# In-projection and state space part woven with attention in steps of at most six products

## The chip, the cores and the metric

The kernel runs on one core of one Trainium2 chip. The core has five engines, each with its own queue of instructions that it works off in order: TensorE (PE, matrix products and transposes; its weight loads are shown apart as PEld), VectorE (DVE), ScalarE (ACT), GpSimd (POOL) and SyncE (SP), which here issues nearly all DMA transfers. Engines wait for each other by semaphores. The metric is the device time of one execution in microseconds (us); the time of a kernel is the median of its runs.

## The reference

Two layers of a transformer with 1024 tokens of width 1024, in float32. A layer modulates and normalises its input, multiplies it by w_in (2472 columns) and feeds three heads in parallel: differential attention (4 heads, q and k of width 32, v of width 64), latent attention (MLA, 4 heads, from a normalised c_q and c_kv) and a state space part (8 heads, state 64, a causal convolution of width 4 ahead of it, a gate z behind it). The three outputs are joined, multiplied by w_out and added to the input; then comes an MLP of 4096 with the square of relu.

```python
def _diff_attention(q, k, v, lam, subln_g, lambda_init):
    ...
        p = _masked_softmax(s1, mask) - lam * _masked_softmax(s2, mask)
        return jnp.einsum('bhqk,bkhe->bqhe', p.astype(v.dtype), v)
    ...
def _ssd_scan(xs, dt, a, bm, cm):
    ...
    scores = jnp.einsum('bclhn,bcshn->bhcls', cc, bc) * decay_in
    y_diag = jnp.einsum('bhcls,bcshp->bclhp', scores, xd)
    ...
    def step(state, inp):
        st, dec = inp
        return state * dec[..., None, None] + st, state
    ...
    y_off = jnp.einsum('bclhn,bchpn,bhcl->bclhp', cc, prev, jnp.exp(a_cs))
    return (y_diag + y_off).reshape(b, l, h, p)
```

## The kernel before

**Products.** A float32 product is made of three products of split operands (a high part and a remainder): `mm3` (L190 to L193) issues high by high, high by low and low by high into one PSUM bank. A bank of the in-projection holds 512 columns for 128 rows and sums over 8 tiles of 128, so it takes 24 products, and then ACT or DVE empties it.

**The part that is woven.** `mixer` runs the in-projection together with both attentions. Each of these is a Python generator that writes down instructions and, between them, yields a cost:

- `in_proj` writes q, k, v, then the columns for MLA (they go to HBM as the tensor d_c), then those of the state space part (xbc) with their convolution, up to the mark "pairs". Behind that comes the z loop over 8 tiles of 128 tokens: a bank of z columns, then `scores`, `first` and `second` of the state space part for that tile (L1255 are the Y products of `second`, L1263 those with the state, L1273 the new state). It reaches "hidden" ahead of the last `second`.
- `attention` goes through four heads of differential attention. Scores are L962 and L964, the softmax L896 and L897, the transposes of the probabilities L922, their products with v L909, the turned results L938. When a head is done, it is normalised (L987 to L991) and written to HBM (d_cc, L992).
- `mla` goes through the tiles t of 128 tokens: `first` loads the d_c rows of a tile (L1041), scales them on DVE (L1042, L1043) and transposes them on PE (L1046); `second` multiplies them by the up-projections (L1056, L1058); `third` transposes q and k (L1085). It also reads back the heads' and the state space part's outputs from d_cc (L1146, L1147). `load_wout` loads w_out in eight parts (L1288).

`weave` adds cost / rate to a stream's clock at each yield and lets the stream with the smallest clock go next. There are three weaves in a layer: up to "pairs" with the first two heads; the z loop with the other two heads and the head of MLA; and what is left of the z loop with the first scores of MLA and the load of w_out.

**What sets the order.** The generators set the order in which the program is written. The scheduler of the language then orders each engine's instructions again by its own estimate of when each can start, and that order is what the engines follow. All working tiles come from one arena in on-chip memory, given out in the order of writing: a place that was given back earliest is taken first. So when the order of writing changes, tiles get other places, and a load waits for whoever had its place last, all over the kernel.

**Behind the weave.** The output projection (L1324 to L1330: loads and stores of the residual) runs with MLA and is followed by the MLP. `renorm` normalises a tile and, for the tiles 4 to 7, makes transposes and several sums of them (`transp_late`, L212 on PE, L217 and L231 on DVE) for a Strassen-like product in the MLP. `mlp_up` first does six plain blocks (L315, L317: 24 products each, weights by six narrow loads of 128 columns, 0.5 MB, L270), beside which the last tiles are transposed, and then for each of 16 blocks the products of sums (`sums`), whose weights come by 1-MB loads of 256 columns (L270 again) and are added on POOL (L284 to L290). L230 and L231 split operands on ACT and DVE; L248 stores results to HBM.

The functions that the diff touches, and what calls them:

## Time and profile before

| | before |
|---|---|
| median of 3 runs | 2828.76 us (2823.73 to 2833.22) |
| the profiled execution | 2827.39 us |
| its span, from the first to the last instruction | 2825.7 us |
| PE busy | 2642.5 us, 94% |
| DVE, ACT, POOL busy | 1755.9, 1111.0, 587.5 us |
| mean granted clock of PE, as a share of full speed | 0.952 |

An engine is busy while it executes; register, branch and semaphore instructions and the issuing of DMAs do not count. The granted clock is what a throttle leaves PE of its full clock: a stretch is either at the full 2.4 GHz or at half of it, and a figure between is a mean over stretches. A row of the timeline names the line, the tile written and the tile read; a bracket behind it gives the time for which the engine stood idle just before and who released it.

### The profile page before, as it was taken

The page shows a single profiled execution, that of the slowest core. Times are in us where ns is not written, and L with a number is a line of the kernel's source. Part 1 is how long each engine was busy: PE and PEld are TensorE (multiplying, and loading weights), DVE is VectorE, ACT ScalarE, POOL GpSimd, SP SyncE. Part 2 cuts the span into 40 slices and gives each one's busy share as a digit, 9 for nine tenths or more (in the row PEclk, how much of TensorE's full clock was granted, in tenths as well). Part 3 has the DMA queues.
Part 4 walks back from the last instruction along what each step waited for, and adds up shares of the span by engine and source line. Part 5 has one row for each costly group of instructions (what it writes and reads, how often), then busy time and mean ns, then how long its engine had stood idle before and what let it go on. Part 6 is the DMA issues. An engine that isn't in the chain of part 4 may idle for free.

```text
span 2825.7 us, 34756 instructions
## 1 busy us (share of the span) xinstructions
PE 2642.5 (94%) x12530; PEld 2066.1 (73%) x12530; DVE 1755.9 (62%) x3223; ACT 1111.0 (39%) x2145; POOL 587.5 (21%) x517
## 2 busy tenths in 40 slices
PE   5799999899879999999999999988997999999998
PEld 4677776676757777777778777765766888888886
DVE  7767666544867777756585576664459654643435
ACT  5243443544534446121143433354445455621212
POOL 1441233310333220000021113342003522000002
PEclk9899988899989999999999998888998999999999
DMA  6441212322345546534331121132133432541313
GB/s 225 116 137 51 94 50 61 110 73 84 101 150 165 158 148 216 179 122 151 107 119 48 56 91 63 54 101 86 52 105 104 153 116 101 177 149 65 120 47 102
DMA packets 268527, 311.54 MB, mean 110 GB/s; under 512 B 28674, under 2 KB 212164, under 8 KB 268356
## 3 DMA queue, kind: packets, MB, share of 16 engines
q1 hardware_dynamic: 268356, 309.32, 34.0%
q8 instruction: 99, 1.62, 0.2%
q14 instruction: 72, 0.59, 0.1%
HBM read 242.85 MB, written 66.43 MB: 109 GB/s over the span
## 4 chain that ended last, share of the span: by engine, by line
PE 65%; DVE 11%; DMA 7%; issue 2%; ACT 2%; POOL 1%; SPq 0%; DVEq 0%; ACTq 0%; POOLq 0%
PE bank_b L191 9%; PE bank_b L193 9%; PE bank_b L192 9%; PE bank_s L191 8%; PE bank_s L192 8%; PE bank_s L193 8%; PE bank_s L962 3%; DVE split L231 2%; PE bank_a L909 2%; PE bank_t L922 2%; DVE arena_f L570 2%; DMA arena_f<-in_w_ada 1%; DMA d_r<-arena_f 1%; PE bank_s L656 1%; PE bank_a L938 1%
## 5 line engine op out<-in xcount | busy, mean ns | idle before, releaser
L191 PE MATMUL bank_b<-split 128*128 128x512 f32 (+2 forms) x1824 | 728.5, 400 | 51.0 <-ACT split L230 33.1
L192 PE MATMUL bank_b<-split 128*128 128x512 f32 (+2 forms) x1824 | 709.6, 389 | 3.5 <-DVE split L231 3.1
L193 PE MATMUL bank_b<-split 128*128 128x512 f32 (+2 forms) x1824 | 706.5, 389 | 2.9 <-DVE split L231 2.9
L230 ACT CAST split<-arena_f 128x512 fp32r<-128x512 f32 (+1 forms) x424 | 305.8, 747 | 678.3 <-PE bank_s L192 425.8
L191 PE MATMUL bank_s<-split 128*128 128x512 f32 (+2 forms) x1152 | 456.1, 398 | 18.3 <-DVE arena_f L390 6.7
L192 PE MATMUL bank_s<-split 128*128 128x512 f32 (+2 forms) x1152 | 451.2, 392 | 4.4 <-DVE split L231 1.8
L191 PEld LDWEIGHTS bank_b<-split 128*128 128x128 f32 x1824 | 354.1, 194 | 129.5 <-ACT split L230 34.8
L193 PE MATMUL bank_s<-split 128*128 128x512 f32 (+2 forms) x1152 | 448.2, 389 | 0.0
L231 DVE TENSOR_TENSOR split<-arena_f,split 128x512 fp32r<-128x512 f32 (+1 forms) x424 | 381.7, 919 | 92.8 <-ACT split L230 92.0
L193 PEld LDWEIGHTS bank_b<-split 128*128 128x128 f32 x1824 | 352.7, 193 | 71.6 <-DVE split L231 5.0
L192 PEld LDWEIGHTS bank_b<-split 128*128 128x128 f32 x1824 | 354.7, 194 | 68.5 <-issue 4.9
L408 DVE TENSOR_TENSOR arena_f<-arena_f,bank_s 128x1024 f32<-128x1024 f32 x126 | 153.5, 1218 | 230.9 <-PE bank_s L193 230.9
L191 PEld LDWEIGHTS bank_s<-split 128*128 128x128 f32 (+1 forms) x1152 | 218.4, 190 | 73.8 <-DVE arena_f L390 7.4
L192 PEld LDWEIGHTS bank_s<-split 128*128 128x128 f32 (+1 forms) x1152 | 219.5, 191 | 50.4 <-DVE split L231 3.5
L193 PEld LDWEIGHTS bank_s<-split 128*128 128x128 f32 (+1 forms) x1152 | 219.1, 190 | 43.4 <-issue 0.2
L897 ACT ACTIVATE arena_f<-bank_s,nm 128x128 f32<-128x128 f32 (+3 forms) x192 | 141.8, 740 | 191.8 <-DVE nm L896 160.8
L896 DVE TENSOR_REDUCE nm<-bank_s 128x1 f32<-128x128 f32 (+3 forms) x192 | 142.2, 752 | 118.8 <-PE bank_s L1111 64.5
L570 DVE SCALAR_TENSOR_TENSOR arena_f<-arena_f,cond 128x128 f32<-128x128 f32 x448 | 161.7, 387 | 71.4 <-DMA arena_f<-in_b_ada 32.9
L246 ACT ACTIVATE arena_f<-arena_f 128x512 f32<-128x512 f32 x128 | 80.8, 632 | 141.6 <-DVE arena_f L331 69.6
L962 PE MATMUL bank_s<-split 32*128 32x512 f32 (+3 forms) x576 | 124.0, 390 | 12.3 <-ACT arena_f L897 9.1
L925 ACT COPY arena_f<-bank_t 128x512 f32<-128x512 f32 (+1 forms) x160 | 86.8, 542 | 114.1 <-PE bank_t L922 100.9
L696 POOL TENSOR_TENSOR arena_f<-arena_f 128x1024 f32<-128x1024 f32 x14 | 33.6, 2399 | 454.0 <-ACT rstd_y L182 340.0
(281 smaller groups left out, 3207.0 us busy)
## 6 DMA issues: line engine op xcount, KB each, us to landing
arena_f<-in_w_ada SPq DMA_DIRECT2D x80, 512.0 KB
d_r<-arena_f SPq DMA_DIRECT2D x128, 256.0 KB
arena_f<-in_w_up SPq DMA_DIRECT2D x32, 1024.0 KB
arena_f<-in_w_down SPq DMA_DIRECT2D x64, 512.0 KB
arena_f<-d_r SPq DMA_DIRECT2D x64, 512.0 KB
arena_f<-d_x SPq DMA_DIRECT2D x36, 512.0 KB
d_x<-arena_f SPq DMA_DIRECT2D x23, 512.0 KB
arena_f<-in_w_in SPq DMA_DIRECT2D x20, 512.0 KB
```

Of the source, the lines that this page charges most:

```text
L191: mm(out, wh, xh, start=start, stop=False)
L192: mm(out, wh, xl, start=False, stop=False)
L193: mm(out, wl, xh, start=False, stop=stop)
L230: self.nc.scalar.copy(hi, src)
L231: (eng or self.nc.vector).tensor_sub(lo, src, f32(hi))
L246: nc.scalar.activation(t, t, AF.Relu)
L408: nc.vector.tensor_add(y[t], y[t], ps)
L570: nc.vector.scalar_tensor_tensor(acc, in0=w[:, k], scalar=self.cond[:, k:k + 1], in1=acc, op0=ALU.mult, op1=ALU.add)
L896: nc.vector.tensor_reduce(nm, S[:, 0:n], axis=AX.X, op=ALU.max, negate=True)
L897: nc.scalar.activation(p[:, 0:n], S[:, 0:n], AF.Exp, bias=nm, accum_out=ls)
L925: nc.scalar.copy(held, ps[:, 0:w])
L962: nc.tensor.matmul(S[mp][:, c0:c1], Q[rw, a, tok], K[rw, b, c0:c1], start=a == b, stop=a == 1 and c1 < n)
```

## The change

The products of an in-projection bank are no longer written in one piece. `feat_major` and `tok_major` become generators that yield 1.3 after every two of the eight tiles summed, that is after six products (`values` after twelve, at a quarter of the width). The yield after the bank falls from 5.1 to 1.2, so a bank costs 3 x 1.3 + 1.2 = 5.1 as before; the two yields of 4.6 of a d_c tile become 2.6. `second` yields 1.0 five times, of which four lie inside it, in place of 5.0 behind it. The part ahead of "attend" is not woven, and its background work is called at the same places as before. Two rates change: attention 80 to 76 in the second weave, the rest of the z loop 1 to 1000 in the third.

```diff
@@ feat_major, tok_major
     def feat_major(self, wt, m, hT, hf):
         ps = self.bank()
...
         for k in range(KD):
             self.mm3(ps, wt[:, 0, k, mm], wt[:, 1, k, mm], hT[0][:, k, sl], hT[1][:, k, sl], k == 0, k == KD - 1)
+            if k % 2 and k < KD - 1:
+                yield 1.3
         return ps

-    def tok_major(self, wt, hT, t, n):
-        ps = self.bank()[:, 0:n]
+    def tok_major(self, wt, hT, t, ps, step=2):
         sl = slice(t * P, t * P + P)
         for k in range(KD):
             self.mm3(ps, hT[0][:, k, sl], hT[1][:, k, sl], wt[:, 0, k], wt[:, 1, k], k == 0, k == KD - 1)
-        return ps
+            if (k + 1) % step == 0 and k < KD - 1:
+                yield 1.3
@@ qk, values
-                yield 5.1
+                yield 1.2
...
-                ps = self.tok_major(wt, hT, t, 256)
+                ps = self.bank()[:, 0:256]
+                yield from self.tok_major(wt, hT, t, ps, 4)
...
                 if t % 2:
                     next(bg, None)
-                    yield 5.1
+                yield 1.3
@@ in_proj: C_CQ tiles (twice), xbc, z loop
-            yield 4.6
+            yield 2.6
...
-                ps = self.feat_major(wt, m - m0, hT, hf)
+                ps = yield from self.feat_major(wt, m - m0, hT, hf)
...
-                yield 5.1
+                yield 1.2
...
-            for k in range(KD):
-                self.mm3(ps, hT[0][:, k, tok], hT[1][:, k, tok], wz[:, 0, k], wz[:, 1, k], k == 0, k == KD - 1)
+            yield from self.tok_major(wz, hT, t, ps)
             z = F.get(512)
...
-            yield 5.1
+            yield 1.2
             held = scores(t, held)
...
-            second(t, z, held)
-            yield 5.0
+            yield from second(t, z, held)
+            yield 1.0
@@ second
             for h in range(8):
                 nc.tensor.matmul(yd[:, h * 64:h * 64 + 64], L[:, h], xd[:, h], start=True, stop=True)
+                if h == 3:
+                    yield 1.0
             nc.vector.tensor_add(y, y, yd.rearrange("p (h e) -> p h e", e=64))
+            yield 1.0
...
                 F.put(xs)
+            yield 1.0
...
                 nc.vector.tensor_add(state, state, sp.rearrange("p (h e) -> p h e", e=64))
+            yield 1.0
@@ mixer
-        self.weave((80, da), (80, self.until(ip, "hidden")), (20, self.until(m, "hidden"), PRE))
-        self.weave((1, ip), (30, self.until(m, 0)), (WOW, self.load_wout(l, st)))
+        self.weave((76, da), (80, self.until(ip, "hidden")), (20, self.until(m, "hidden"), PRE))
+        self.weave((1000, ip), (30, self.until(m, 0)), (WOW, self.load_wout(l, st)))
```

In the changed kernel the lines from L900 on are about 5 higher, from L1279 on 10 higher: the load of d_c L1041 is L1046 there, the write of a head L992 is L997, the reads of d_cc L1146 and L1147 are L1151 and L1152, the write of the state space part L1279 is L1289, the load of w_out L1288 is L1298, the residual's stores and loads L1330 and L1346 are L1340 and L1356.

SP's queue in layer 1, where the weave ends and MLA begins, before (d_cc_116<-arena_f 128x8x64 is the write of head 3, the first 128x384 load of d_c behind it is that of tile 3):

```order
L1279 DMA d_cc_116<-arena_f 128x512
L1288 DMA arena_f<-in_w_out 128x1024 x3
L992 DMA d_cc_116<-arena_f 128x8x64
L1146 DMA arena_f<-d_cc_116 128x2x256
L1041 DMA arena_f<-d_c_114 128x384
L1146 DMA arena_f<-d_cc_116 128x2x256
L1147 DMA arena_f<-d_cc_116 128x2x512
L1041 DMA arena_f<-d_c_114 128x384
```

And after (the first two 128x384 loads belong to tiles 2 and 3, the pair to tiles 5 and 4):

```order
L1289 DMA d_cc_116<-arena_f 128x512
L1046 DMA arena_f<-d_c_114 128x384
L1298 DMA arena_f<-in_w_out 128x1024 x5
L1046 DMA arena_f<-d_c_114 128x384
L1289 DMA d_cc_116<-arena_f 128x512
L1298 DMA arena_f<-in_w_out 128x1024
L1152 DMA arena_f<-d_cc_116 128x2x512
L1046 DMA arena_f<-d_c_114 128x384 x2
L997 DMA d_cc_116<-arena_f 128x8x64
L1151 DMA arena_f<-d_cc_116 128x2x256
```

The loads of tiles 3, 4 and 5 have moved ahead of the write of the head. In layer 0 it is the other way round. SP's queue there before (the second 128x384 load is that of tile 3, the third that of tile 4):

```order
L1041 DMA arena_f<-d_c_113 128x384
L1288 DMA arena_f<-in_w_out 128x1024
L1041 DMA arena_f<-d_c_113 128x384
L1288 DMA arena_f<-in_w_out 128x1024 x3
L627 DMA arena_f<-d_mod 128x8x1
L1288 DMA arena_f<-in_w_out 128x1024
L992 DMA d_cc_115<-arena_f 128x8x64
L1041 DMA arena_f<-d_c_113 128x384
```

And after (the single 128x384 load is that of tile 5, the pair is tiles 3 and 4):

```order
L1289 DMA d_cc_115<-arena_f 128x512
L1046 DMA arena_f<-d_c_113 128x384
L561 DMA arena_f<-in_b_ada 1x128
L997 DMA d_cc_115<-arena_f 128x8x64
L1151 DMA arena_f<-d_cc_115 128x2x256
L1046 DMA arena_f<-d_c_113 128x384 x2
L1152 DMA arena_f<-d_cc_115 128x2x512
```

The load of tile 3 has moved behind the write of the head and its reading back.

SP's queue in layer 0 where the MLP begins, before (128x8x128 are the narrow loads, of which the first and the second row here are the fifth and the sixth; of the 128x8x256 loads the single one is block 1, the four are blocks 2, 0, 3 and 4):

```order
L270 DMA arena_f<-in_w_up 128x8x128
L248 DMA d_r_109<-arena_f 128x512 x3
L270 DMA arena_f<-in_w_up 128x8x128
L1330 DMA d_x_104<-arena_f 128x1024
L248 DMA d_r_109<-arena_f 128x512 x2
L270 DMA arena_f<-in_w_up 128x8x256
L248 DMA d_r_109<-arena_f 128x512
L270 DMA arena_f<-in_w_up 128x8x256 x4
L248 DMA d_r_109<-arena_f 128x512 x2
```

And after (the 128x8x256 loads are blocks 1, 0 and 2 in that order, the narrow one between them is the sixth):

```order
L270 DMA arena_f<-in_w_up 128x8x128 x2
L248 DMA d_r_109<-arena_f 128x512
L1340 DMA d_x_104<-arena_f 128x1024
L248 DMA d_r_109<-arena_f 128x512 x2
L270 DMA arena_f<-in_w_up 128x8x256
L566 DMA arena_f<-in_norm_g 1x128
L561 DMA arena_f<-in_b_ada 1x128
L248 DMA d_r_109<-arena_f 128x512
L270 DMA arena_f<-in_w_up 128x8x256
L270 DMA arena_f<-in_w_up 128x8x128
L248 DMA d_r_109<-arena_f 128x512
L270 DMA arena_f<-in_w_up 128x8x256
```

Block 0's load has moved from third to second place of the wide ones and ahead of the sixth narrow one. On PE, the last transposes of `transp_late` in that layer stood directly ahead of the first products of `sums`; they now stand ahead of the 24 products of the sixth plain block, and 36 products behind the transposes of tile 6. On POOL, three sets of L284, L285, L287 stood ahead of the first L290; now one does. In layer 1, where the MLP begins, the queue has the last two narrow loads ahead of three stores (L248) instead of behind them, with block 0's wide load ahead of both.

## Rows read from the trace of the kernel before

**Rows 1.** The page: busy time, share of the span, instructions of each engine.

```profile
PE 2642.5 (94%) x12530; PEld 2066.1 (73%) x12530; DVE 1755.9 (62%) x3223; ACT 1111.0 (39%) x2145; POOL 587.5 (21%) x517
```

**Rows 2.** Busy time by window: engines, clock, DMA share, GB/s; z parts, one stretch.

```profile
336.00:476.00 140.00, 135.90 (x645) 99.66 (x645) 99.63 (x225) 57.50 (x137) 49.25 (x35) 0.84 0.21 64
1724.00:1884.00 160.00, 153.58 (x739) 111.34 (x739) 107.85 (x248) 64.62 (x154) 59.85 (x43) 0.87 0.21 64
360.00:380.00 20.00, 20.00 (x63) 15.10 (x62) 14.07 (x36) 6.54 (x15) 6.43 (x6) 0.52 0.23 72
```

**Rows 3.** Timeline of PE (start, us, operation): whole banks at full and half clock.

```profile
767.67 0.39 PE L192 MATMUL bank_b<-split 128*128 128x512 f32 x1
...
772.66 0.39 PE L193 MATMUL bank_b<-split 128*128 128x512 f32 x1
...
376.07 0.63 PE L193 MATMUL bank_b<-split 128*128 128x512 f32 x1
...
378.63 0.63 PE L193 MATMUL bank_b<-split 128*128 128x512 f32 x1
```

**Rows 4.** Timeline of SP's queue, layer 1, from weave to MLA.

```profile
1912.25 0.38 SPq L992 DMA_DIRECT2D d_cc<-arena_f  x1
1914.88 0.38 SPq L1146 DMA_DIRECT2D arena_f<-d_cc  x1
1915.31 0.46 SPq L1041 DMA_DIRECT2D arena_f<-d_c  x1
```

**Rows 5.** Timeline of PE at the same place.

```profile
1919.19 0.90 PE L1046 MATMUL bank_t<-ident,arena_f 128*128 128x128 f32 x3 [8.74 <-DVE arena_f L1042]
```

**Rows 6.** Timeline of SP's queue and of PE, layer 0, from weave to MLA.

```profile
500.81 0.32 SPq L1041 DMA_DIRECT2D arena_f<-d_c  x1
...
519.73 0.38 SPq L992 DMA_DIRECT2D d_cc<-arena_f  x1
...
518.86 0.55 PE L1046 MATMUL bank_t<-ident,arena_f 128*128 128x128 f32 x3
```

**Rows 7.** Timeline of PE, layer 0, where the MLP begins.

```profile
774.89 0.50 PE L191 MATMUL bank_b<-split 128*128 128x512 f32 x1 [1.84 <-ACT split L230]
...
778.32 0.79 PE L193 MATMUL bank_b<-split 128*128 128x512 f32 x1 [1.69 <-DVE split L231]
...
784.78 1.04 PE L212 MATMUL bank_s<-ident,arena_f 128*128 128x128 f32 x8
804.84 0.79 PE L191 MATMUL bank_b<-split 128*128 128x512 f32 x1 [19.02 <-ACT split L230]
```

**Rows 8.** Timeline of SP's queue at the same place.

```profile
770.14 0.38 SPq L270 DMA_DIRECT2D arena_f<-in_w_up  x1
...
785.85 0.38 SPq L270 DMA_DIRECT2D arena_f<-in_w_up  x1
...
792.27 1.01 SPq L270 DMA_DIRECT2D arena_f<-in_w_up  x2
```

**Rows 9.** Timeline of DVE (the last remainders of L212's transposes) and POOL there.

```profile
790.74 2.96 DVE L231 TENSOR_TENSOR split<-arena_f,split 128x512 fp32r<-128x512 f32 x3
...
791.70 1.44 POOL L284 TENSOR_TENSOR arena_f<-arena_f 128x512 f32<-128x512 f32 x1 [16.17 <-DMA arena_f<-in_w_up]
...
801.53 1.26 POOL L284 TENSOR_TENSOR arena_f<-arena_f 128x512 f32<-128x512 f32 x1
```

**Rows 10.** Timelines of PE and SP's queue, layer 1, where the MLP begins.

```profile
2167.50 0.50 PE L191 MATMUL bank_b<-split 128*128 128x512 f32 x1 [4.56 <-ACT split L230]
...
2170.05 0.79 PE L193 MATMUL bank_b<-split 128*128 128x512 f32 x1 [0.81 <-DVE split L231]
...
2185.60 0.79 PE L191 MATMUL bank_b<-split 128*128 128x512 f32 x1 [7.65 <-ACT split L230]
...
2162.15 0.38 SPq L270 DMA_DIRECT2D arena_f<-in_w_up  x1
```

More of the change, by code (lines that the diff above doesn't have):

```diff
@@ L775, in qk @@
                 s = 32.0 ** -0.5 if i == 0 else 1.0
-                ps = st["qk0"][i][:, hf * 512:hf * 512 + 512] if m == 0 and "qk0" in st else self.feat_major(wt, i, hT, hf)
+                if m == 0 and "qk0" in st:
+                    ps = st["qk0"][i][:, hf * 512:hf * 512 + 512]
+                else:
+                    ps = yield from self.feat_major(wt, i, hT, hf)
                 e = st["qk"][m][i][:, :, hf * 512:hf * 512 + 512]
@@ L798, in in_proj @@
         for hf in range(2):
-            for n, c in enumerate(qk(0, w0, hf)):
-                next(late, None)
-                yield c
-            for c in values(w1, range(hf * 4, hf * 4 + 4)):
-                next(late, None)
-                yield c
+            for c in qk(0, w0, hf):
+                if c != 1.3:
+                    next(late, None)
+            for n, _ in enumerate(values(w1, range(hf * 4, hf * 4 + 4))):
+                if n % 4 == 3:
+                    next(late, None)
         yield "attend"
@@ L811, in in_proj @@
             tok = slice(t * P, t * P + P)
-            for k in range(KD):
-                self.mm3(ps, hT[0][:, k, tok], hT[1][:, k, tok], wt[:, 0, k], wt[:, 1, k], k == 0, k == KD - 1)
+            yield from self.tok_major(wt, hT, t, ps)
             e, j = F.get(424), F.get(424)
@@ L823, in in_proj @@
             next(bg, None)
-            yield 4.6
+            yield 2.6
             next(bg, None)
-            yield 4.6
+            yield 2.6
         ssm = self.ssm(l, st)
@@ L873, in in_proj @@
             ps = self.bank()
-            tok = slice(t * P, t * P + P)
-            for k in range(KD):
-                self.mm3(ps, hT[0][:, k, tok], hT[1][:, k, tok], wz[:, 0, k], wz[:, 1, k], k == 0, k == KD - 1)
+            yield from self.tok_major(wz, hT, t, ps)
             z = F.get(512)
```

## Prediction

> **What bounds the kernel now.** I read the page first: TensorE (PE) is busy for 94% of the span, the next engine for 62% [rows 1]. So a microsecond is won only where PE stands still or where it runs slowly. Next I cut the span into stages (busy time by window) and asked for PE's idle time and clock in each. The woven stretch is nearly full: in the part where the z columns are woven, PE is busy 135.9 of 140 us in layer 0 and 153.6 of 160 us in layer 1 [rows 2], and a bank of in-projection products stands there without gaps. Between the first and the last of 23 products in a row lie 22 steps of (772.66 - 767.67) / 22 = 0.227 us at the full clock, and (378.63 - 376.07) / 6 = 0.427 us at the half [rows 3]. The mean granted clock of the two z parts is 0.84 and 0.87 [rows 2], so they lose more to the clock than to waiting. What is left to win by order alone inside the weave is about 4 + 6 us.
>
> Then I looked for single long waits of PE outside, in the timeline. Three kinds stand out, all at joins where the woven streams hand over, and all of them end with a DMA that SP issued late because something ahead of it in SP's queue waited. (1) Layer 1, start of the latent attention (MLA): 8.74 us at 1919.19, for the normalised d_c rows of tile 3 [rows 5]. (2) Layer 0, start of the MLP: 1.84, 1.69 and 19.02 us [rows 7]. (3) Layer 1, start of the MLP: 4.56, 0.81 and 7.65 us [rows 10].
>
> **The change part by part.** *Counts.* The order of the changed kernel has on every engine the instructions of before and no more; a yield costs the chip nothing. The costs of a bank add up as before (3 x 1.3 + 1.2 = 5.1), so the streams keep their pace; the rates 76 and 1000 only shift who goes next. Term: 0.
>
> *Steps of six products.* What is written in steps is not what PE sees, since the scheduler orders each engine's instructions again afterwards. I counted runs of in-projection products between other PE work in the order: 47 before and 49 after in layer 0's z part, 58 and 65 in layer 1's, most of them still 16 to 24 products long, and the long stretches of scores, transposes and state products between them keep their length. The half-clock stretches follow those; PE's idle time there, 10 us together, is a ceiling [rows 2]. I take 0 for the weave itself, with ends of -10 (all of that idle gone) and +10 (one more stretch at half clock, of 20 us as from 360 to 380 us, where the mean is 0.52 [rows 2]: it holds 47 products of 0.427 us, which would take 10.7 us at 0.227, so 9.3 us are lost [rows 3]).
>
> *The five steps of second().* Its eight Y products, the state product and the vector work are no longer one block; nothing is added, and the same queue of PE work covers them. Term 0, inside the bounds just given.
>
> *The d_c loads, layer 1.* Before, SP reaches the write of head 3 (L992) at 1912.25 us, waits for it to land before L1146 at 1914.88, and only then issues tile 3's load at 1915.31 [rows 4]; the vector engine (DVE) scales the rows as soon as they land, and PE goes on at 1919.19, 3.9 us after the issue [rows 5]. In the new order tile 3's load, and those of tiles 4 and 5, stand ahead of the head's write. Then the transposes wait for nothing that the profile shows: -8.7 us.
>
> *The d_c loads, layer 0.* The order does the opposite here. Before, tile 3's load was issued at 500.81, 19 us ahead of the head's write at 519.73 [rows 6]. Now it stands behind that write and behind the reading back of it. PE came to tile 3's transposes at 518.86 [rows 6], 0.9 us ahead of the head's write, and the new order has about as much PE work there (4 us of scores and transposes more, 5.5 us of Y and state products less). So PE would be there 1 to 2 us ahead of the write; the read follows 2.6 us behind the write, the load 0.4 us behind the read, and PE's work 3.9 us behind the load [rows 4, 5]: a wait of 8 to 9 us. I take + 8.7, the wait of layer 1: what leaves one layer appears in the other. Both together: 0, bounds -8.7 (the new wait is covered) to + 8.7 (layer 1 keeps its wait).
>
> *MLP start, layer 0.* The wait of 19.02 us has this chain [rows 7 to 9]: the last transposes of the stream (L212, tile 7) at 784.78, directly ahead of the sums; the load of block 1 waits for them and goes at 785.85; block 0, which the first sum needs, is third in the group of 792.27; GpSimd (POOL) works them off in the order of landing, block 0 at 801.53; PE starts at 804.84. In the new order block 1's load waits for tile 6 only and block 0's stands next, before the sixth narrow load, and a whole narrow block (24 products, 5.5 us) lies between the last transposes and the sums. POOL's first set of sums is then block 0's. So the sums find their weights. But the sixth narrow load now stands behind block 0's and needs an arena place that the remainders of an earlier tile leave. One such chain took from 784.78 to 793.70 (8.9 us) [rows 7, 9]; two interleave here, for which I estimate between the one chain's time and half as much again, 9 to 13 us. From issue to the first product it took 774.89 - 770.14 = 4.75 us [rows 7, 8], so PE has that block 13.7 to 17.8 us after the transposes of tile 6, and has work until then for 36 x 0.227 + 2 x 1.04 = 10.3 us. It waits 3.4 to 7.5 us; I take 7.5, the 1.7 us of the split that follows as now, and 1 us at the sums: 10.2 in place of 22.5. Term: -12.4. Ends: -19 (3.4 us and nothing else), and -5 (the sums keep a wait of 7.65 us as layer 1's do [rows 10]).
>
> *MLP start, layer 1.* The 4.56 us come from a narrow load issued at 2162.15 behind three stores [rows 10]. In the new order the last two narrow loads stand ahead of those stores, with some 20 us of products ahead of their use. The 4.56 and the 0.81 us go: -5.4. The last transposes still stand directly before the sums, so the 7.65 us stay. Ends: -9 (some 16 products behind that wait, which run at the half clock after it, would take 0.227 in place of 0.427 us) and + 3 (block 0's 1-MB load now goes ahead of the narrow ones and holds them).
>
> **Sum.** 0 + 0 - 12.4 - 5.4 = -17.8 us. The profiled execution took 2827.4 us (span 2825.7, the rest lies around it), 1.4 us under the median of 2828.8. So 2827.4 - 17.8 = 2809.6, say 2810 us.
>
> **The rivals.** *Nothing moves* (27%). The scheduler has regrouped the products already, and a late load at a join is a lottery of arena places: the sixth narrow block waits as long as the sums did. For it speaks that the z part's order is hardly altered and that the d_c wait shows up in the other layer; against it that the two MLP starts really have their loads earlier in SP's queue. Time: 2827 us.
>
> *The clock falls more often* (15%, the slower side). Half-clock stretches now follow 20 us of short products of scores and state, as at 360 to 380 us [rows 2], and PE comes back to 0.227 us a product after some 5 us of in-projection products [rows 3]. If banks cut in four make those returns come later, each z part gets two more such stretches, 4 x 9.3 = 37 us: 2847 us. It decides from three stretches on (2810 + 28 = 2838). The place is the z parts, the sign a mean clock there of 0.75 instead of 0.84. Against it: most runs still hold 16 to 24 products. The Trainium skill (TensorE: Matmul & The Clock Gate, section "Loop structure matters more than you think") speaks for this rival: all k-products of an output tile belong back to back. By that rule a bank cut into four would run slower than a whole one; the trace shows whole banks at the full clock, and none that is cut by intent.
>
> **How the numbers follow.** A measurement of this kernel can tell about 0.3% from no change, so faster means under 2820.3 and slower over 2837.2 us. The forecast (58%) has its own range from 2793 (-12.4 and -5.4 at their good ends, -5 for the weave, -3 for the joins) to 2820. The middle case holds 27%, the slower one 15%. The range of 8 in 10 reaches from 2793 over the middle case with its + 7 of bounds to 2834.
>
> **What would show it.** The wait before the first sum in layer 0 is under 3 us, and one of 3 to 8 us stands a block earlier; the wait of 4.56 us in layer 1 is gone; tile 3's d_c load goes ahead of the head's write in layer 1, and PE's idle time at the MLA start is some 9 us less there and some 9 us more in layer 0; the clock of the z parts stays within 0.03 of 0.84 and 0.87. I am wrong if the z parts change their length by more than 10 us, or if the sums of layer 0 still wait over 10 us: then the order of loads was not what held them.

## The result and the profile after

The changed kernel takes 2798.6 us (median of 4 runs, 2796.5 to 2799.95) against 2826.2 us of the kernel before on the same chip (4 runs, 2820.7 to 2833.2): a ratio of 0.990, with an interval of 0.987 to 0.993. It is faster by 27.6 us, or 1.0%. The profiled execution took 2798.41 us (span 2796.6), at a mean granted clock of 0.956 in place of 0.952. The page's first row after answers to [rows 1]:

```profile
PE 2621.3 (94%) x12530; PEld 2049.1 (73%) x12530; DVE 1749.1 (63%) x3223; ACT 1110.3 (40%) x2145; POOL 583.9 (21%) x517
```

PE executes as many instructions as before and is busy for 21 us less; some 16 us of that are clock (the ledgers below). I cut both traces at the same instructions of PE and compared the stretches. "Before" is one profile; a second one (e9) differs from it by up to 2.2 us a stretch, and by 5 us in the first down-projection. "After" is the mean of four profiles: the changed kernel twice (it and e5) and e6 and e7 below, whose times don't differ from its own beyond the noise.

| stretch of PE (us) | layer 0: before, difference | layer 1: before, difference | forecast |
|---|---|---|---|
| z part: its first scores to its last state product | 176.3, -7.7 | 170.4, -6.5 | 0, 0 (+-10) |
| MLA start: from there to the last d_c transposes | 95.0, +10.4 | 109.9, -6.8 | +8.7, -8.7 |
| from there to the last turned result (L938) | 101.9, 0 | 97.9, +2.5 | 0, 0 |
| MLP start: from there to the down-projection | 392.5, -21.0 | 358.5, -5.6 | -12.4, -5.4 |
| down-projection (in layer 1 to the end) | 414.3, -1.9 | 358.0, +7.6 | 0, 0 |
| the rest, up to the z part | 333.9, +3.0 | 208.3, -0.5 | 0, 0 |

They add up to -26.5 us. The work in a stretch is nearly the same: up to 14 instructions of PE have moved across a cut. Now the joins, one after the other. **MLA start, layer 1.** SP's queue, as in [rows 4]:

```profile
1869.88 0.33 SPq L1046 DMA_DIRECT2D arena_f<-d_c  x1
...
1876.29 0.80 SPq L1046 DMA_DIRECT2D arena_f<-d_c  x2
1883.13 0.37 SPq L997 DMA_DIRECT2D d_cc<-arena_f  x1
```

The loads of the d_c rows (L1041 before, L1046 now) go 6 us and more ahead of the head's write (L992 before, L997 now), and the 8.74 us of [rows 5] are gone. **MLA start, layer 0.** SP's queue, then PE, as in [rows 6]:

```profile
525.44 0.38 SPq L997 DMA_DIRECT2D d_cc<-arena_f  x1
528.03 0.37 SPq L1151 DMA_DIRECT2D arena_f<-d_cc  x1
528.45 4.51 SPq L1046 DMA_DIRECT2D arena_f<-d_c  x2
```

```profile
531.69 0.90 PE L1051 MATMUL bank_t<-ident,arena_f 128*128 128x128 f32 x3 [7.27 <-DVE arena_f L1047]
```

Here the load now goes 3.0 us behind the head's write, and PE stands for 7.27 us. The wait has moved from one layer to the other. **MLP start, layer 0.** PE, as in [rows 7], and the split on ACT that it waits for; then SP's queue, as in [rows 8]; then POOL, as in [rows 9]:

```profile
765.42 1.03 PE L212 MATMUL bank_s<-ident,arena_f 128*128 128x128 f32 x8
...
774.47 1.04 PE L212 MATMUL bank_s<-ident,arena_f 128*128 128x128 f32 x8
786.99 0.79 PE L191 MATMUL bank_b<-split 128*128 128x512 f32 x1 [11.49 <-DVE arena_f L217]
...
790.38 0.79 PE L193 MATMUL bank_b<-split 128*128 128x512 f32 x1 [1.31 <-DVE split L231]
...
799.49 0.39 PE L191 MATMUL bank_b<-split 128*128 128x512 f32 x1
```

```profile
786.32 1.66 ACT L230 CAST split<-arena_f 128x512 fp32r<-128x512 f32 x3 [0.91 <-DMA arena_f<-in_w_up]
```

```profile
767.17 0.38 SPq L270 DMA_DIRECT2D arena_f<-in_w_up  x1
...
779.31 2.18 SPq L270 DMA_DIRECT2D arena_f<-in_w_up  x2
```

```profile
784.73 1.69 POOL L284 TENSOR_TENSOR arena_f<-arena_f 128x512 f32<-128x512 f32 x1 [6.59 <-DVE arena_f L318]
...
792.21 1.67 POOL L290 TENSOR_TENSOR arena_f<-arena_f 128x512 f32<-128x512 f32 x1 [2.43 <-DVE split L231]
```

Block 0's load goes at 779.31 and the sixth narrow one behind it; both are issued by 779.31 + 2.18 = 781.5. POOL's first set of sums is block 0's; the products of sums, from about 799.5 on, follow without a wait. PE waits a block earlier instead, 11.49 + 1.31 us at the sixth narrow block, in place of 1.84 + 1.69 + 19.02. PE's row names L217, but ACT splits the weights of that block only from 786.32 on, when their load has landed, and PE starts at 786.99; in e5, e6 and e7 the row names this split. **MLP start, layer 1.** PE, as in [rows 10]:

```profile
2146.14 1.94 PE L212 MATMUL bank_s<-ident,arena_f 128*128 128x128 f32 x8 [6.85 <-DVE arena_f L639]
2152.09 1.95 PE L191 MATMUL bank_b<-split 128*128 128x512 f32 x3 [4.01 <-ACT split L230]
...
2169.34 0.47 PE L191 MATMUL bank_b<-split 128*128 128x512 f32 x1 [1.37 <-ACT split L230]
```

The 4.56 us are gone, but PE now waits 6.85 us for the row of the last tile ahead of its transposes; the 7.65 us at the sums became 4.01. **Two waits that were not there**, both of PE in layer 1, at the z part and at the down-projection:

```profile
1747.80 1.12 PE L1235 MATMUL bank_t<-ident,arena_f 128*128 128x128 f32 x4 [8.13 <-ACT arena_f L930]
...
2439.37 0.79 PE L191 MATMUL bank_s<-split 128*128 128x512 f32 x1 [5.92 <-ACT arena_f L406]
```

**Two ledgers.** From each trace I took PE's idle time and the time in which it was busy at the half clock. A product of a row of banks takes 0.227 us at the full clock and 0.427 at the half [rows 3], so a microsecond of work at the half clock would have taken 0.53 us at the full, and 1 - 0.227 / 0.427 = 0.47 us of it are lost. All 14 profiles of this case fit: last end on PE = 2541 + idle + 0.47 x (busy at half clock), to within 5 us. Idle and half-clock time were 174 and 212 us before, 167 and 177 after. For the runs without a profile the granted clock gives the time at the half clock as 2 x (1 - clock) x span, PE's idle time at that clock included: 266 us in the mean of 31 runs of the kernel before (standard deviation 15), 243 us in 17 of the changed kernel, e6 and e7 (standard deviation 11). On the chip of e5 to e7 alone it is 270 us in 14 runs and 244 in 13.

### The profile page after: what moved, and what is told of

Its sections match the earlier page's. It is cut to its first block, busy times and chain, and to the rows that moved or that the text cites. A ratio compares the mean times of both kernels' runs of the same rounds, so it can differ in the third digit from the quotient of the medians.

```text
span 2796.6 us, 34697 instructions
## 1 busy us (share of the span) xinstructions
PE 2621.3 (94%) x12530; PEld 2049.1 (73%) x12530; DVE 1749.1 (63%) x3223; ACT 1110.3 (40%) x2145; POOL 583.9 (21%) x517
## 4 chain that ended last, share of the span: by engine, by line
PE 59%; DVE 5%; DMA 2%; ACT 2%; issue 1%; POOL 1%; DVEq 0%; SPq 0%; ACTq 0%; POOLq 0%
PE bank_b L191 9%; PE bank_b L193 9%; PE bank_b L192 9%; PE bank_s L191 8%; PE bank_s L192 8%; PE bank_s L193 8%; PE bank_s L967 1%; PE bank_a L914 1%; DVE split L231 1%; PE bank_t L927 1%; DVE arena_f L639 1%; PE bank_t L581 1%; PE bank_b L1260 1%; ACT split L230 0%; PE bank_a L943 0%
## 5 line engine op out<-in xcount | busy, mean ns | idle before, releaser
L191 PEld LDWEIGHTS bank_b<-split 128*128 128x128 f32 x1824 | 349.8, 192 | 108.7 <-ACT split L230 19.5
L193 PEld LDWEIGHTS bank_b<-split 128*128 128x128 f32 x1824 | 348.5, 191 | 69.5 <-issue 3.9
L192 PEld LDWEIGHTS bank_b<-split 128*128 128x128 f32 x1824 | 349.5, 192 | 64.3 <-issue 4.6
L191 PEld LDWEIGHTS bank_s<-split 128*128 128x128 f32 (+1 forms) x1152 | 218.0, 190 | 81.8 <-ACT arena_f L902 10.1
L902 ACT ACTIVATE arena_f<-bank_s,nm 128x128 f32<-128x128 f32 (+4 forms) x192 | 142.1, 742 | 163.6 <-DVE nm L901 119.7
L246 ACT ACTIVATE arena_f<-arena_f 128x512 f32<-128x512 f32 x128 | 81.0, 633 | 109.9 <-DVE arena_f L331 51.3
L967 PE MATMUL bank_s<-split 32*128 32x512 f32 (+3 forms) x576 | 117.1, 386 | 7.4 <-ACT arena_f L902 5.1
```

Source lines behind the costliest of these rows:

```text
L191: mm(out, wh, xh, start=start, stop=False)
L192: mm(out, wh, xl, start=False, stop=False)
L193: mm(out, wl, xh, start=False, stop=stop)
L246: nc.scalar.activation(t, t, AF.Relu)
L902: nc.scalar.activation(p[:, 0:n], S[:, 0:n], AF.Exp, bias=nm, accum_out=ls)
L967: nc.tensor.matmul(S[mp][:, c0:c1], Q[rw, a, tok], K[rw, b, c0:c1], start=a == b, stop=a == 1 and c1 < n)
```

## The experiments

Two theories stood against each other. **A**: the gain sits at the joins; new places in the arena and the two rates moved a few loads. **B**: the finer steps themselves help, by a denser PE in the weave. Ratios are to the kernel before on the same chip, with 95% intervals.

**e1_rate76_only: a rate alone, no steps.**

```diff
-        self.weave((80, da), (80, self.until(ip, "hidden")), (20, self.until(m, "hidden"), PRE))
+        self.weave((76, da), (80, self.until(ip, "hidden")), (20, self.until(m, "hidden"), PRE))
```

> The kernel before with whole banks and an undivided second(); of the change only the rate 76 in place of 80 for attention in the second weave. Theory A (the time is won at the joins, by which arena places and queue positions the loads happen to get; the steps are only one way to shuffle them): the shuffle alone moves the time. In this order tile 3's d_c load stands behind the head's write and takes the head's own place in both layers, so layer 0 should get a wait of 7 to 9 us at its MLA start and layer 1 keep its 8.7; at the MLP start of layer 0 block 0's load no longer stands behind the last transposes, so the 19.0 us should shrink to 7 to 9. Sum about 2826 + 8 - 11 = 2823 us. Theory B (finer steps let PE run fuller and at a higher clock in the z parts): nothing of the step is here, so the z parts keep 176 and 170 us and the time stays at 2826.

2811.8 us (10 runs), ratio 0.995 [0.993, 0.998]. PE at the MLA starts of both layers and at the first MLP start:

```profile
524.47 0.90 PE L1046 MATMUL bank_t<-ident,arena_f 128*128 128x128 f32 x3 [9.11 <-DVE arena_f L1042]
...
1916.34 0.91 PE L1046 MATMUL bank_t<-ident,arena_f 128*128 128x128 f32 x3 [10.22 <-DVE arena_f L1042]
```

```profile
774.92 0.80 PE L191 MATMUL bank_b<-split 128*128 128x512 f32 x1 [4.82 <-ACT split L230]
793.56 0.80 PE L191 MATMUL bank_b<-split 128*128 128x512 f32 x1 [10.02 <-ACT split L230]
```

Other places, other waits: the d_c wait now in both layers, the 19.02 us down to 10.02. So a rate alone, without any step, moves the time by 11 us, 0.4 of what the change gave. The sum of waits that I had expected (2823 us) was 11 us too slow.

**e2_proj_steps: the changed kernel with `second` in one piece.** Its inner yields are taken out and 5.0 yielded behind it, as before.

```diff
-            yield from second(t, z, held)
-            yield 1.0
+            second(t, z, held)
+            yield 5.0
...
```

> The changed kernel with second() written in one piece again (yield 5.0 behind it); the steps of six products and both new rates stay. Theory A: what counts is the new shuffle: tile 3's load has a place of its own and stands ahead of the head's write in both layers (no wait of 7 to 9 us at either MLA start), block 0's wide load is the first in both layers, the last transposes stand directly ahead of the sums in layer 0 (a wait of 7 to 8 us there) and 24 products ahead of them in layer 1. About 2826 - 9 - 11 - 8 = 2798 us, the same as the changed kernel by other means. Theory B with the steps of second() as the cause: z parts back to 176 and 170 us, about 2798 + 11 = 2809 us; with the steps of the products as the cause: 2798.

2804.4 us (10 runs), ratio 0.993 [0.991, 0.996]. There is no d_c wait in either layer, but in layer 0 PE stands at the MLA start for another stream:

```profile
532.30 0.90 PE L927 MATMUL bank_t<-ident,arena_f 128*128 128x128 f32 x3 [6.28 <-ACT arena_f L1054]
```

Its 151 us of idle time are the least of all, 16 us less than in the changed kernel, and it takes some 5 us more: the profiled execution, one of its slower ones (2813.2 us), spent 234 us busy at the half clock. Idle time that goes is no gain by itself. Both z parts are as long as before in that profile (172.2 and 172.5 us, after 176.3 and 170.4), where the changed kernel has 171.6 and 164.2. The time lies between the 2798 of theory A and the 2809 that I had given B with the steps of `second` as the cause, so it decides for neither.

**e3_before_dc_top: the kernel before, d_c rows taken from the other end of the arena**, so that they share no place with a head's output.

```diff
-            cn = F.get(384)
+            cn = F.get(384, top=True)
```

> The kernel before; only the d_c row tiles of MLA get their arena place from the other end (from the top), so that none shares the place of the head that is being written. Theory A: tile 3's load stands ahead of the head's write in both layers, the 8.74 us of layer 1 go, none appears in layer 0; the places behind shift too: block 0's load becomes the first wide one in layer 0, so the 19.0 us become 7 to 9. About 2826 - 9 - 11 = 2806 us with nothing of the change in it. Theory B: 2826 - 9 = 2817 at most, and the z parts as before.

2824.7 us (10 runs), ratio 1.000 [0.997, 1.002]: a miss. The d_c wait is gone in layer 1, but PE waits at the same place for the softmax:

```profile
1905.20 0.58 PE L191 MATMUL bank_s<-split 96*128 96x256 f32 x1 [4.36 <-ACT arena_f L897]
...
1918.14 1.11 PE L909 MATMUL bank_a<-arena_f 128*64 128x256 f32 x4 [4.91 <-ACT arena_f L925]
```

At this MLA start idle time fell from 17.5 to 14.6 us only, and over the whole execution from 174 to 170. (The 236 us busy at the half clock in the profile, after 212, are those of the slowest of ten executions, 2833 us; over all ten the granted clock gives 266 us at the half clock, as before.) A wait of one stream at a join is partly what another stream would wait for anyway.

**e4_before_block0_top: the kernel before, block 0's place at the other end**, so that its load waits for no earlier tile.

```diff
-                st = F.get(KD, 2 * P if sums else P)
+                st = F.get(KD, 2 * P if sums else P, top=sums and i == 0)
```

> The kernel before; only the first wide load of w_up (block 0 of the sums, in each layer) takes its arena place from the top. Up to the MLP of layer 0 the program is word for word that of before. In the order, block 0's load goes from third of the wide ones to first, ahead of the sixth narrow load, and 20 products stand between the last transposes and the sums. Theory A: the 19.02 us at the start of the sums shrink to 3 to 8 us, the sixth narrow block waits 2 to 6 us longer, layer 0 wins 8 to 14 us; layer 1 within 5 us. About 2814 us. If the load of block 0 was not what held the sums (rival: POOL's sums or the transposes' remainders hold them), the wait stays above 15 us: 2826.

2818.4 us (10 runs), ratio 0.998 [0.996, 0.999]. PE at the MLP start of layer 0:

```profile
765.12 0.79 PE L191 MATMUL bank_b<-split 128*128 128x512 f32 x1 [3.98 <-DVE rstd_t L185]
768.94 1.94 PE L212 MATMUL bank_s<-ident,arena_f 128*128 128x128 f32 x8 [1.75 <-DVE arena_f L639]
...
781.06 1.22 PE L191 MATMUL bank_b<-split 128*128 128x512 f32 x2 [2.55 <-ACT split L230]
```

The 19.02 us are gone, so it was block 0's late load that held the sums. The whole is 5 to 6 us faster; other waits of 2 to 4 us take over, and in layer 1 the places have moved too, so that the d_c wait of 8.74 us is gone there and others stand elsewhere (idle time in all 174 to 159 us). Up to the MLP of layer 0 this kernel's instructions stand on every engine as in the kernel before, which makes the first z part a test of the clock. Busy time by window, columns as in [rows 2], in this kernel, in the kernel before profiled once more (e9) and in the changed kernel profiled once more (e5):

```profile
336.00:476.00 140.00, 133.43 (x721) 97.59 (x721) 106.41 (x247) 62.05 (x149) 53.98 (x39) 0.96 0.23 71
```

```profile
336.00:476.00 140.00, 136.78 (x660) 100.22 (x656) 99.57 (x228) 58.32 (x139) 49.42 (x35) 0.85 0.20 64
```

```profile
336.00:476.00 140.00, 134.61 (x660) 98.40 (x659) 98.10 (x229) 58.41 (x138) 50.16 (x36) 0.89 0.21 62
```

The same instructions ran at a granted clock of 0.96 here and of 0.84 and 0.85 in the two profiles of before. The whole z part took 162.9 us with 15 us at the half clock here, 176.3 with 49 and 177.9 with 51 there.

**e5_after_again and e9_before_again: both kernels once more, unaltered.**

> The changed kernel, unaltered, for more executions of it and for a second profile of the same program. If the half-clock stretches were set by the program, the two z parts would again take 171.6 and 164.2 us with 44 and 34 us at the half clock. If they are chance from one execution to the next (the fourth run's layer 0 had the program of before and 163 us with 15 us at the half clock where before had 176 and 49), the z parts differ by 5 to 15 us between the two profiles of this program, and the median of ten executions lies within 8 us of 2799; the waits (7.3 us for d_c in layer 0, 11.5 us at the MLP start of layer 0, 6.9 and 4.0 us in layer 1) come back within 1 us.

> The kernel before, unaltered, for a second profile of the same program. If the half clock in the z parts is chance, the z parts differ from 176 us (49 at half) and 170 us (41 at half) by several us each way, while the waits come back within 1 us: 8.7 us for d_c in layer 1, 19.0 us at the sums of layer 0, 4.6 and 7.7 us in layer 1. If the program sets it, all of these come back.

e5: 2800.6 us (5 runs), ratio 0.991 [0.988, 0.995]; e9, one run, 2832.2 us. The waits come back: e9 has 19.11, 8.84 and 4.63 us in place of 19.02, 8.74 and 4.56, and idle time is 173.9 us after 174.2 in before, 166.3 after 166.8 in the changed kernel. The first z part of the changed kernel took 171.6 us in one profile and 166.1 in the other. Layer 1's came back: 164.2 and 163.8 us, each with 24 us busy at the half clock (and 164.2 with 24 once more in e10 below), where the two profiles of before have 170.4 and 172.5 us with 41 and 46. So waits belong to the program, while half-clock time varies with the execution and belongs in part to the program as well.

**e6_steps_of_12 and e7_steps_of_3: the changed kernel with steps of twice and of half the size.** e6 yields 3.9 once in the middle of a bank. e7 yields 0.557 behind every tile summed:

```diff
-            if k % 2 and k < KD - 1:
-                yield 1.3
+            if k < KD - 1:
+                yield 0.557
...
```

> The changed kernel with one yield of 3.9 in the middle of a bank in place of three of 1.3: steps of twelve products; the bank's cost is the same 5.1. In the order all loads at the joins have the places and neighbours that they have in the changed kernel. Theory A (places and queue positions at the joins): the same time as the changed kernel, within 6 us, with the same waits at the joins. Theory B (the finer the steps the fuller the z parts): it loses part of the gain, 5 to 12 us slower than the changed kernel.

> The changed kernel with a yield of 0.557 after every three products (7 x 0.557 + 1.2 = 5.1): twice as fine. The loads at the joins again have the places that they have in the changed kernel. Theory A: the same time as the changed kernel within 6 us. Theory B: another 3 to 10 us faster than it; with the rule that all products of a bank belong back to back: 5 us or more slower, by more half clock in the z parts.

2798.8 us and 2796.1 us (4 runs each), ratios 0.990 [0.985, 0.995] and 0.990 [0.986, 0.994]. PE at the MLP start of layer 0, e6 and then e7:

```profile
787.24 0.80 PE L191 MATMUL bank_b<-split 128*128 128x512 f32 x1 [10.83 <-ACT split L230]
```

```profile
784.42 0.80 PE L191 MATMUL bank_b<-split 128*128 128x512 f32 x1 [11.54 <-ACT split L230]
```

The size of the step is indifferent between 12 and 3 products: theory B falls for the products of a bank. For the steps of `second`, which both kernels keep, it is open (e2). In layer 0's z part the z products stand in 14 uninterrupted runs on PE when a bank is written whole, in 13 when cut in two, in 14 when cut in four or in eight; in layer 1's in 16, 14, 19 and 19. The scheduler puts them together again, in layer 1 not wholly. So the rule of the Trainium skill that the prediction weighed (TensorE: Matmul & The Clock Gate, section "Loop structure matters more than you think"), matmuls of a tile back to back, is hardly tested by this change. (The page sets this against a wait for a DMA between the matmuls, not against other products between them.) Where the banks are cut up more, in layer 1, the trace shows no loss: with 19 runs the z part was busy at the half clock for 24, 24 and 19 us, with 16 for 41 and 46, with 14 for 41.

**e8_after_dc_top: the changed kernel with e3's edit.** It was to take away the 7.27 us in layer 0.

```diff
-            cn = F.get(384)
+            cn = F.get(384, top=True)
```

> The changed kernel; only the d_c row tiles of MLA take their place from the top, so that tile 3's load in layer 0 no longer takes the place of the head that is being written. In the order the load stands ahead of the head's write in both layers. Theory A: the wait of 7.3 us at the MLA start of layer 0 goes, to 0 to 3 us of other waits, the MLP start of layer 0 keeps its 11.5 us (its loads have the same neighbours); about 5 us under the changed kernel. If another wait takes its place (the softmax, as in the third run, where the d_c wait went and waits of 4 to 5 us for the softmax came), the time stays.

2835.7 us (10 runs), ratio 1.004 [1.001, 1.006]: some 35 us slower than the changed kernel, where I had expected 5 us less. The wait went, and both MLA starts are about 9.5 us shorter. But far behind it PE now stands at the MLP start of layer 1, and in layer 0 it stops over and over inside the up-projection:

```profile
2188.67 0.80 PE L191 MATMUL bank_b<-split 128*128 128x512 f32 x1 [16.62 <-ACT split L230]
```

```profile
863.86 0.47 PE L191 MATMUL bank_b<-split 128*128 128x512 f32 x1 [1.35 <-DVE arena_f L331]
...
876.89 0.47 PE L191 MATMUL bank_b<-split 128*128 128x512 f32 x1 [1.36 <-DVE arena_f L327]
```

From the last transposes to the down-projection layer 0 takes 328.1 us (30.8 idle) in place of 307.7 (15.2 idle). In layer 1 three sets of sums (L284, L285, L287) again stand on POOL ahead of the first L290, as in layer 0 of the kernel before. Waits are only part of the loss: idle time rose from 167 to 182 us, the time busy at the half clock from 177 to 206. One edit of one tile's place is worth between -9.5 us at its own join and +35 us in all.

**e10_after_dc_on_act: the changed kernel, d_c loads issued by ACT**, which has no head's write ahead of them.

```diff
-            nc.sync.dma_start(cn, self.d_c[l][t * P:t * P + P, 0:384])
+            nc.scalar.dma_start(cn, self.d_c[l][t * P:t * P + P, 0:384])
```

> The changed kernel; only the d_c loads of MLA are issued from ScalarE's queue instead of SyncE's. Arena places are the same: tile 3's load in layer 0 still goes to the place from which the head is being written. If the position in SP's queue is what made PE wait (my forecast's step), the load no longer stands behind the write and its reading back: the 7.3 us in layer 0 go to under 2 us. If the shared place is the cause, the load still has to wait until the write has read the place: the wait shrinks by the 0.4 us of SP's issue at most and by the 2.6 us of the reading back if that can be passed, so it stays at 4 to 7 us, and ScalarE, which now stands behind the load, loses time too.

One run, 2819.2 us, which is too little to compare times. SP's queue, ACT's queue and PE at the MLA start of layer 0:

```profile
530.17 0.38 SPq L997 DMA_DIRECT2D d_cc<-arena_f  x1
532.76 0.38 SPq L1151 DMA_DIRECT2D arena_f<-d_cc  x1
```

```profile
532.76 0.39 ACTq L1046 DMA_DIRECT2D arena_f<-d_c  x1
```

```profile
536.60 0.90 PE L1051 MATMUL bank_t<-ident,arena_f 128*128 128x128 f32 x3 [7.50 <-DVE arena_f L1047]
```

With another queue the load still goes 2.6 us behind the head's write, at the moment at which that has landed, and PE waits 7.50 us. It isn't the place in SP's queue that holds it, but its place in the arena: the head's output is still being read from there.

**e11_pick1 and e12_pick2: two versions picked by where their loads stand in the order.** e12 is the changed kernel with d_c rows at the other end and the last rate at 1 again; e11 has `second` in one piece and `load_wout` at 24 in place of 16 as well.

```diff
-            cn = F.get(384)
+            cn = F.get(384, top=True)
...
-        self.weave((1000, ip), (30, self.until(m, 0)), (WOW, self.load_wout(l, st)))
+        self.weave((1, ip), (30, self.until(m, 0)), (WOW, self.load_wout(l, st)))
```

> Picked by the order alone: the changed kernel with second() in one piece, d_c places from the top, the rate 1 in the third weave and 24 for the load of w_out. In its order tile 3's d_c load stands ahead of the head's write in both layers and shares no place with it, block 0's wide load is the first wide one in both layers and needs no place of the last transposes, and in layer 1 two narrow blocks (48 products) stand between the last transposes and the sums; in layer 0 none. Theory A: no d_c wait in either layer, at the sums 5 to 8 us in layer 0 (the transposes' remainders) and under 2 us in layer 1: about 10 us under the changed kernel, 2785 to 2795 us. If the joins are not what counts: between 2799 and 2826.

> The second pick by the order: the changed kernel with d_c places from the top and the rate 1 in the third weave. Tile 3's load ahead of the head's write in both layers, block 0's wide load ahead of the fifth narrow one in layer 0 and first of the wide ones in layer 1, 44 products between the last transposes and the sums in layer 0 and none in layer 1. Theory A: no d_c wait, under 3 us at the sums of layer 0, 7 to 8 us at those of layer 1: 2785 to 2795 us.

2827.3 us and 2810.5 us (10 runs each), ratios 1.001 [0.998, 1.004] and 0.996 [0.994, 0.998]: misses, where I had expected 2785 to 2795. PE at the MLP start of layer 0 in e11, then in e12:

```profile
802.52 1.94 PE L212 MATMUL bank_s<-ident,arena_f 128*128 128x128 f32 x8 [8.23 <-DVE arena_f L639]
808.47 1.95 PE L191 MATMUL bank_b<-split 128*128 128x512 f32 x3 [4.01 <-ACT split L230]
```

```profile
774.82 0.79 PE L191 MATMUL bank_b<-split 128*128 128x512 f32 x1 [7.47 <-ACT split L230]
```

The loads stood where I wanted them, and other waits came: 8.23 us ahead of the last transposes in e11, 7.47 us at a narrow block in e12. The profiled executions were busy at the half clock for 260 us in e11 (its slowest run, 2851 us) and for 227 in e12 (with 157 us idle). No version that ran beats the changed kernel clear of the noise.

**What theory A is worth.** It foresaw which load stands ahead of which, and mostly where PE then waits. As a sum of waits it missed the time in e1, e3, e8, e11 and e12, by 11 to some 40 us: other waits take over, the clock moves, and a new order of writing changes places far behind the join.

**Left open.** Steps with the old rates, and whole banks with both new rates, weren't run. So whether a cut in a bank at these very rates is worth anything against no cut isn't measured; that it doesn't matter whether there is one cut, three or seven, is. What the five steps of `second` are worth isn't known either: e2 takes them out, but moves the joins too.

## Why the prediction was right, and where it wasn't

The forecast of 2810 us was 11 us too slow; direction, joins and range held.

- **Steps, 0 +- 10 us.** The size was off. The order of layer 0 is as foreseen, 14 runs before and after; layer 1 has 19 in place of 16. (My 47, 49, 58 and 65 runs can't be runs of z products, most of them 16 to 24 long: a z part has 8 x 24 = 192 products.) PE's idle time in the z parts went from 8.8 to 6.4 us and from 6.4 to 10.9 us, and yet the parts are 14 us shorter together, more than the -10 that I had as the end and as a sign of being wrong. In layer 0, chance alone makes 13 us of one z part (e4 against before), so its 7.7 us can't be put down to the change. In layer 1 the part took 164.2, 163.8, 164.2 and 163.2 us in the four profiles of after, in spite of the 8.13 us wait in three of them, and 170.4 and 172.5 in the two of before: these 6 to 9 us come back and belong to the change; by which of its parts isn't shown. The idle time was no ceiling, since the clock could win too, and one half-clock stretch of 9.3 us was no bound on what a single execution loses.
- **The d_c loads, -8.7 and +8.7.** Right in both layers: 8.74 to 0 and 0 to 7.27 us; the stages moved by -6.8 and +10.4. The wait was 1.4 us smaller than my 8.7: PE came 1.0 us ahead of the write and went on 3.2 us behind the load, where I had 3.9. The step that gave the reason failed: I read "behind the head's write in SP's queue" as the cause, and e10 shows that the shared place in the arena is.
- **MLP start, layer 0, -12.4.** The mechanism was right point by point: block 0 first on POOL, no wait at the sums, a wait a block earlier. (Before, block 0 was third of the wide loads, not third in the group of 792.27, where it is the second.) The size of that wait was off: 11.49 us, where I took 7.5. I had 9 to 13 us from tile 6's transposes to the sixth narrow load; with block 0's load, which itself went after 779.31 - 765.42 = 13.9 us, ahead of it, it went after nearly 16. From there to PE's first product it took some 5.5 to 6 us, with a megabyte under way ahead of it, where I had 4.75. Nevertheless the stage won 21 us, more than my end of -19. Its three waits fell by 22.55 - 12.80 = 9.75 us, where I had 12.4; the rest lies around them, at places for which I had no term. In the profile of the changed kernel the stage has 17.4 us less idle time, and it is busy at the half clock for 10.1 us less, which is worth another 4.7 us. The stretch ahead of the first L212 has 4.6 us less idle time, and of four waits of 1.3 to 2.0 us inside the up-projection one of 1.5 is left.
- **MLP start, layer 1, -5.4.** The total of -5.6 is right by luck, out of two errors. The 4.56 us went, as forecast, but I took the 7.65 us at the sums to stay, and they became 4.01, while 6.85 us came ahead of the last transposes, which I had not looked for.
- **Not foreseen:** the down-projection of layer 1, +7.6 us, with the 5.92 us shown above among it and 3.4 us busy at the half clock where before had none; the wait comes back with 4.1 to 5.7 us in e5, e6 and e7. I had followed no load behind the MLP start.
- **The rivals.** "The clock falls more often" is out: 177 us busy at the half clock after, 212 before, and over all runs 243 us at the half clock in the mean in place of 266. Of the 28.6 us between the first two profiles, 7.4 are idle time and 0.47 x 34.7 = 16 are clock; some 5 us are neither. These 5 us come back: the constant is 2538, 2538, 2537 and 2538 us in the four profiles of after and 2543 and 2544 in the two of before, and what they are is open. The clock part isn't chance in the main, since 266 - 243 = 23 us is six times the error of that difference (3.8 us, from the two standard deviations). Some of it comes from layer 1's z part (24 us in place of 41); elsewhere fewer waits, after which PE starts at the half clock, as behind the 11.49 us above, are a reason that was not tested. "Nothing moves" was half right: a lottery of arena places it was, but with a prize.

## What to carry to other kernels

Don't credit an idea with what the new layout of memory gives or takes: vary the size of the idea (steps of 12, 6 and 3), and do its side effects alone (a rate), before you believe in it. Where a load is late, ask which buffer it gets and who read that last, before you ask what stands ahead of it in its queue; and count on another stream's wait behind the one that you remove. Idle time can be compared from two profiles, time at the half clock only over ten or more runs (here its standard deviation was 11 to 15 us a run).

## What the runs showed of the hardware

The same instructions in the first z part spent 15 to 51 us at the half clock from one execution to the next, which made that part 162.9 to 177.9 us long; in the second z part of the changed kernel, 24 us at the half clock came back in three executions. PE's idle time over a whole execution came back to within 1 us in each of the two kernels that were profiled twice. The wait for a place in memory was the same through another engine's DMA queue: 7.27 us from SP, 7.50 us from ACT.
